# A first mixer whose gate row and next modulation move to ScalarE and GpSimd, and whose second output projection takes split weights

## Chip, core and metric

The kernel runs on one core of one Trainium2 chip. The metric is the device time of one execution in microseconds (us), lower is better. TensorE is called PE here, VectorE DVE, ScalarE ACT, GpSimd POOL, and SyncE, which issues nearly all loads, SP.

## What is computed

Two transformer blocks run one after the other on 256 tokens of width 1024. The change touches only the front of the first one:

```python
shift, scale, gate = ada_modulation(c, ada_w[l, s], ada_b[l, s])   # silu(c) @ w + b, in three parts; gate is 1 + the third
h = x * (1 + scale) + shift
y = mixer_ab(h, ...)                    # two attentions side by side, concatenated, @ w_out
x = layer_norm(alpha * x + gate * y, ...)
shift, scale, gate = ada_modulation(c, ada_w[l, s + 1], ada_b[l, s + 1])
h = x * (1 + scale) + shift             # enters the first MLP
```

mixer_ab holds a sliding-window attention ("a", with sinks) and a top-64 attention ("b"): for "b" an index score picks 64 keys for each token, and those scores must be finished before its mask exists. Both outputs, 512 columns each, go through one 1024x1024 projection. Everything is fp32.

## The kernel before

**Weights** come in chunks of 128x2048 fp32 (1 MB). Class Stream keeps them in one list in the order of use. A load is issued on SP up to three chunks ahead into one of four buffers "raw"; a chunk is then taken apart in pieces when the program needs it (need, get). Three kinds of chunk matter. A split chunk is turned into whi on ACT (L157, a rounded copy) and wlo on DVE (L158, the rest), and a product then takes three fp32r matmuls (L227 whi with x high, L228 wlo with x high, L229 whi with x low). A native chunk (f32=True) is loaded straight into buffers and multiplied in fp32 (L234). A modulation chunk has the transposed ada weights, and ada_piece (L436) multiplies 128x1024 of it by the row csil = silu(c) and sums along the row, in one DVE instruction.

**The order** on each engine is fixed when the program is built: a scheduler merges the pieces with the work around them. hold says that some chunks' pieces are issued only after a given instruction, here after the second selection mask.

**The front of the program** goes so. Modulation 0 (shift and scale) is summed on DVE. The projections in0, uq, in1 follow. Then come the index scores: six scores on PE, relu on ACT (L907, tile rl), weighted sums into isc on DVE (L913). select takes the 64 best by eight rounds of MAX (L925) and MATCH_REPLACE (L928) for each of two token tiles and ends with the mask smask (L947). Twelve attention units follow, six of "b" and six of "a". A unit is scores (L490, L496), a row maximum on DVE (L498), exponentials on ACT (L509), scaling on DVE (L526), transposes (L534), an evacuation on ACT (L536) and the product with v (L544, L549). Window's work for "a" (projection in2, keys, rope) stands after the first unit.

**The gate row** of modulation 0 is made on PE before: ada_products (L444) multiplies each 1024-wide gate row chunk, cut in four strips, by the column ccol; 32 calls of four strips' matmuls gather eight chunks in one PSUM tile. ada_gate adds the bias (L452, tile grow), spreads the row over the partitions by eight fp32 matmuls (L457) and writes the tile gate (L459). **Modulation 1** (chunks ada 1,0 to 1,7) is 16 DVE instructions L436. The layer norm after the mixer needs gate; the transposes behind it need modulation 1.

**The output projection** (out_proj) runs the half of "b" first, with split chunks about 2 and 3. These products fill PE between the units. The half of "a", chunks about 0 and 1, is native: 16 fp32 products L234 at the end of the mixer, held back by tail so that token tile 0 is finished first.

Of the kernel before, what the change touches and what calls it, by code (L numbers as in the profile page):

```python
# [8 lines left out]
F32 = DT.float32  # L9
# [187 lines left out]
class Kern:  # L197
# [242 lines left out]
    def ada_products(self, raw, ps, kt, o, n):  # L440

        def pc():
            for g in range(4):
# [4 lines left out]
    def ada_gate(self, ps, gate):  # L448

        nc = self.nc  # L450
        row = self.pa.tile([128, 256], F32, tag="grow", name="grow", bufs=1)
        nc.vector.scalar_tensor_tensor(row, ps[:, 0:256], 1.0, self.gate_b, op0=ALU.add, op1=ALU.add)  # L452
        for h in range(2):
            p = self.ps("o")
            for q in range(2):
                g = 32 * (2 * h + q)
                nc.tensor.matmul(p[:, q * 256:q * 256 + 256], self.ident[:, g:g + 1].to_broadcast([128, 128]),  # L457
                                 row, start=True, stop=True)
            nc.scalar.activation(gate[:, h * 512:h * 512 + 512], p, AF.Copy, scale=1.0 / ALPHA)  # L459
# [295 lines left out]
    def mixer_ab(self, gate, early):  # L755
# [3 lines left out]
        for i in range(2):  # L759
# [9 lines left out]
        self.ccol = self.pa.tile([128, KT, 32], F32, tag="ccol", name="ccol")  # L769
        nc.gpsimd.tensor_tensor(self.ccol, self.col("c", 0, 8)[:, :, None].to_broadcast([128, KT, 32]),  # L770
                                e[:, :, None].to_broadcast([128, KT, 32]), op=ALU.mult)
        self.gate_b = self.pa.tile([128, 256], F32, tag="gate_b", name="gate_b")
# [13 lines left out]
        for kt in range(KT):  # L786
# [19 lines left out]
            for t in range(2):  # L806
                k = kt % 4
                self.mm(p0[t][:, :456], (xT[:, kt, t * 128:t * 128 + 128],), wt, slice(k * 456, k * 456 + 456),
                        kt == 0, kt == KT - 1)

# [42 lines left out]

        def keysT(src, kT):

            nc.gpsimd.memset(kT[0:64, :, 1, :], 0.0)
            nc.gpsimd.memset(kT[64:128, :, 0, :], 0.0)
# [26 lines left out]
        kTb = self.px.tile([128, 2, 2, 256], F32, tag="tm", name="kTb", bufs=8)  # L884
        keysT(kd, kTb)
# [67 lines left out]
        def unit(t, heads, qk, mask, scale, v, op, base, done, sink=None):  # L953
# [4 lines left out]
            def s2(pT):  # L958
# [4 lines left out]
                if heads[-1] == 7:  # L963
                    ts = slice(t * 128, t * 128 + 128)
                    p3 = op[0].rearrange("p (a b) -> p a b", a=4)
                    if base == 1:
                        if base not in oT:
                            oT[base] = [self.px.tile([128, 4, 256], F32R, tag="tm", name=self.nm("oT"), bufs=8)
                                        for _ in range(2)]
                        self.split_evac(oT[base][0][:, :, ts], oT[base][1][:, :, ts], p3)  # L970
                    else:
                        if base not in oT:
                            oT[base] = [self.px.tile([128, 4, 256], F32, tag="tm", name=self.nm("oT"), bufs=8)]
                        nc.scalar.activation(oT[base][0][:, :, ts], p3, AF.Copy)
# [32 lines left out]
        for g in range(4):  # L1007
            nc.sync.dma_start(self.gate_b[32 * g:32 * g + 32, :],
                              A["rows"][ROWS["gate_b"]:ROWS["gate_b"] + 1, 256 * g:256 * g + 256].to_broadcast([32, 256]))
# [46 lines left out]
        def hook(i):  # L1056
            if i == 0:
                window()
                S.need(S.index["ada00g", 3])
            if i == 5:  # L1060
                self.ada_gate(self.strips, gate)
# [558 lines left out]
    def schedule_items(self):  # L1620
# [15 lines left out]
        def strips():  # L1636

            if self.strips is None:
# [325 lines left out]
```

## Time and profile before

| | us |
|---|---|
| runs, median (lowest to highest of 3) | 1337.09 (1335.97 to 1338.56) |
| the profiled execution | 1336.42 |
| its span in the trace | 1334.5 |
| PE busy in the span | 1289.8 (97%) |
| DVE busy | 1006.6 (75%) |
| ACT busy | 708.1 (53%) |
| POOL busy | 43.8 (3%) |

The table is read from the bottom: POOL is nearly idle over the whole span, ACT about half, while PE is busy nearly all the time. Shares of a whole span hide stages, so the argument below goes by stretches of the first 160 us: the profile's slices show PE below nine tenths nowhere but in the first two and the last.

### The profile page before, as it was taken

What the parts mean: (1) busy time and instruction counts of PE and PEld (TensorE: products, weight loads), DVE (VectorE), ACT (ScalarE), POOL (GpSimd) and SP (SyncE); (2) the same over time, 40 slices, a digit from 0 to 9 for tenths busy, and PEclk for the clock granted to TensorE, in tenths of its full rate; (3) what the DMA queues carried; (4) which work ended last, traced back from release to release, by engine and by line L of the source; (5) the groups of instructions that cost most, each with busy time, mean ns of one, the idle gap of its engine ahead of it and who ended that gap; (6) DMA issues with size and microseconds to landing.
All of it is one profiled execution on the core that took longest, in us unless ns stands there. A gap on an engine that the chain in (4) does not pass through costs nothing.

```text
span 1334.5 us, 18965 instructions
## 1 busy us (share of the span) xinstructions
PE 1289.8 (97%) x6970; PEld 1051.4 (79%) x6970; DVE 1006.6 (75%) x2048; ACT 708.1 (53%) x1532; POOL 43.8 (3%) x74
## 2 busy tenths in 40 slices
PE   5899999999999999999999999999999999999997
PEld 2356688888787788888699988888888877888886
DVE  7789999976999698666798778666677555766664
ACT  3245645554566665555543437555566754755552
POOL 2000000000100000000010000000000000000000
PEclk9999999999999999999999999999999999999999
DMA  9639689974457468555343334555534333455530
GB/s 363 252 146 332 248 299 347 343 272 158 180 202 281 158 217 300 188 191 178 109 158 116 138 127 170 188 185 188 189 139 158 126 127 126 174 189 189 190 127 32
DMA packets 39023, 260.21 MB, mean 195 GB/s; under 512 B 4625, under 2 KB 5009, under 8 KB 9362
## 3 DMA queue, kind: packets, MB, share of 16 engines
q1 hardware_dynamic: 38786, 258.47, 53.8%
q8 instruction: 55, 0.90, 0.3%
q0 software_dynamic: 144, 0.52, 0.1%
q14 instruction: 38, 0.31, 0.1%
HBM read 257.93 MB, written 1.05 MB: 194 GB/s over the span
## 4 chain that ended last, share of the span: by engine, by line
PE 73%; issue 11%; DVE 8%; ACT 3%; DMA 3%; POOL 2%; SPq 0%; POOLq 0%; DVEq 0%; ACTq 0%
PE acc L229 11%; PE acc L227 11%; PE acc L228 11%; PE scr L250 6%; PE o L250 6%; PE scr L251 3%; PE o L251 3%; PE scr L496 3%; PE acc L234 2%; DVE wlo L158 2%; DMA raw<-in_ada_dram 2%; PE o L534 1%; PE scr L229 1%; DVE junk L436 1%; POOL sm L258 1%
## 5 line engine op out<-in xcount | busy, mean ns | idle before, releaser
L158 DVE TENSOR_TENSOR wlo<-raw,whi 128x512 fp32r<-128x512 f32 x724 | 471.2, 686 | 129.8 <-ACT whi L157 119.9
L157 ACT ACTIVATE whi<-raw 128x512 fp32r<-128x512 f32 x724 | 418.9, 626 | 211.3 <-PE acc L229 87.7
L227 PE MATMUL acc<-whi,hh 128*128 128x512 f32 x512 | 201.2, 394 | 0.0
L228 PE MATMUL acc<-wlo,hh 128*128 128x512 f32 x512 | 201.2, 393 | 0.0
L229 PE MATMUL acc<-whi,hl 128*128 128x512 f32 x512 | 200.1, 392 | 0.0
L250 PE MATMUL scr<-xT,whi 128*128 128x512 f32 x464 | 166.8, 398 | 0.0
L250 PE MATMUL o<-xT,whi 128*128 128x512 f32 x464 | 166.1, 397 | 0.0
L251 PE MATMUL o<-xT,wlo 128*128 128x256 f32 x464 | 130.5, 281 | 0.0
L251 PE MATMUL scr<-xT,wlo 128*128 128x256 f32 x464 | 130.4, 281 | 0.0
L227 PEld LDWEIGHTS acc<-whi,hh 128*128 128x128 f32 x512 | 96.2, 188 | 22.9 <-ACT hh L737 1.3
L229 PEld LDWEIGHTS acc<-whi,hl 128*128 128x128 f32 x512 | 96.2, 188 | 22.1 <-DVE hl L738 0.8
L436 DVE SCALAR_TENSOR_TENSOR junk<-raw,csil 128x1024 bf16<-128x1024 f32 x88 | 108.6, 1234 | 6.2 <-DMA raw<-in_ada_dram 5.8
L228 PEld LDWEIGHTS acc<-wlo,hh 128*128 128x128 f32 x512 | 96.2, 188 | 18.6
L250 PEld LDWEIGHTS o<-xT,whi 128*128 128x128 f32 x464 | 87.1, 188 | 21.0
L250 PEld LDWEIGHTS scr<-xT,whi 128*128 128x128 f32 x464 | 87.1, 188 | 20.7 <-issue 0.5
L251 PEld LDWEIGHTS scr<-xT,wlo 128*128 128x128 f32 x464 | 87.5, 189 | 2.7 <-issue 0.5
L251 PEld LDWEIGHTS o<-xT,wlo 128*128 128x128 f32 x464 | 87.6, 189 | 0.0
L737 ACT ACTIVATE hh<-f 128x512 fp32r<-128x512 f32 x58 | 36.7, 633 | 86.8 <-DVE f L736 86.7
L731 ACT ACTIVATE r<-scr 128x256 f32<-128x256 f32 x58 | 22.3, 384 | 96.6 <-PE scr L251 96.6
L732 DVE TENSOR_TENSOR r<-scr,r 128x256 f32<-128x256 f32 x58 | 24.6, 424 | 55.7 <-ACT r L731 55.4
L738 DVE TENSOR_TENSOR hl<-f,hh 128x512 fp32r<-128x512 f32 x58 | 40.1, 691 | 33.3 <-ACT hh L737 33.1
L229 PE MATMUL acc<-whi,xT 128*128 128x512 f32 (+1 forms) x176 | 63.4, 361 | 0.7 <-DVE xT L306 0.5
(398 smaller groups left out, 2294.9 us busy)
## 6 DMA issues: line engine op xcount, KB each, us to landing
raw<-in_m_w_dram SPq DMA_DIRECT2D x128, 1024.0 KB, 4.8
raw<-in_ada_dram SPq DMA_DIRECT2D x48, 1024.0 KB, 5.4
raw<-in_c_qk_dram SPq DMA_DIRECT2D x8, 1024.0 KB, 4.9
raw<-in_h_qf_dram SPq DMA_DIRECT2D x8, 1024.0 KB, 4.8
raw<-in_mla_o_dram SPq DMA_DIRECT2D x8, 1024.0 KB, 4.8
raw<-in_c_v_dram SPq DMA_DIRECT2D x4, 1024.0 KB, 4.7
raw<-in_c_w_out_dram SPq DMA_DIRECT2D x4, 1024.0 KB, 4.8
raw<-in_h_i_dram SPq DMA_DIRECT2D x4, 1024.0 KB, 5.0
```

What stands on the lines that cost most here:

```text
L157: nc.scalar.activation(hi, raw[:, a:b], AF.Copy)
L158: nc.vector.tensor_tensor(lo, raw[:, a:b], hi.bitcast(F32), op=ALU.subtract)
L227: mm(ps, xh, wh, start=start, stop=False)
L228: mm(ps, xh, wl, start=False, stop=False)
L229: mm(ps, xl, wh, start=False, stop=stop)
L234: self.nc.tensor.matmul(ps, x[0], w(c), start=start, stop=stop)
L250: mm(ps.rearrange("p (a b) -> p a b", a=2), w.h(c), x, start=start, stop=False)
L251: mm(ps[:, n:2 * n], w.l(c), x[:, 0, :], start=False, stop=stop)
L436: nc.vector.scalar_tensor_tensor(junk, raw[:, j * 1024:(j + 1) * 1024], 1.0, self.csil, op0=ALU.mult, op1=ALU.mult, accum_out=acc[:, n:n + 1])
L496: nc.tensor.matmul(o, q, k, start=False, stop=(i == len(ops) - 1))
L737: nc.scalar.activation(hh, f, AF.Copy)
L738: nc.vector.tensor_tensor(hl, f, hh.bitcast(F32), op=ALU.subtract)
```

## The change

Four edits, all in the front of the program:

- The gate row: for each of eight 128x1024 pieces ACT multiplies by one column of ccol (tile prod, two buffers in turn) and POOL adds the result to the tile gate, which is set to 1/32 on 32 partitions and to the bias on one of the others at first. Two fp32 matmuls with a matrix of ones then sum over partitions (ada_gate).
- Modulation 1: for each of 16 pieces POOL multiplies by csil into prod, and ACT copies prod onto itself and sums it. These chunks now stand ahead of the output projection's in the list, and are outside hold.
- Chunks about 0 and 1 are split, and the output of "a" too (split_evac); out_proj takes three fp32r matmuls everywhere.
- The zeroing of the key tiles (POOL) moves ahead of the new POOL work, the need of the gate's chunks ahead of the first attention unit, the need of the last modulation chunk to unit 3, and the bias row's load is one row instead of four broadcasts.

```diff
-    def ada_products(self, raw, ps, kt, o, n):
...
-                self.nc.tensor.matmul(ps()[32 * g:32 * g + 32, 0:n], self.ccol[:, kt, :],
-                                      raw[:, o + g * n:o + g * n + n], start=kt == 0, stop=kt == KT - 1)
+    def ada_rows(self, raw, kts):
...
+                w = self.prod[kt % 2]
+                nc.scalar.activation(w, raw[:, q * 1024:q * 1024 + 1024], AF.Identity, scale=self.ccol[:, kt:kt + 1])
+                nc.gpsimd.tensor_tensor(self.grow, self.grow, w, op=ALU.add)
...
+    def ada_piece2(self, raw, j, acc, n):
...
+            w = self.prod[j]
+            nc.gpsimd.tensor_tensor(w, raw[:, j * 1024:(j + 1) * 1024], self.csil, op=ALU.mult)
+            nc.scalar.activation(w, w, AF.Copy, accum_out=acc[:, n:n + 1])
...
-        row = self.pa.tile([128, 256], F32, tag="grow", name="grow", bufs=1)
-        nc.vector.scalar_tensor_tensor(row, ps[:, 0:256], 1.0, self.gate_b, op0=ALU.add, op1=ALU.add)
...
+            nc.tensor.matmul(p, self.ones, self.grow[:, h * 512:h * 512 + 512], start=True, stop=True)
...
+        self.grow = gate
+        self.prod = [self.pa.tile([128, 1024], F32, tag="prod", name="prod"), self.tm("prod")]
...
-                        nc.scalar.activation(oT[base][0][:, :, ts], p3, AF.Copy)
...
+                    self.split_evac(oT[base][0][:, :, ts], oT[base][1][:, :, ts], p3)
...
-        S.hold(("ada00g", 0), 4, 16, [self.sel_last[1]])
+        S.hold(("about", 2), 0, 16, [self.sel_last[1]])
...
+        keys_zero(kTa)
+        S.need(S.index["ada00g", 3])
...
-                S.need(S.index["ada00g", 3])
+            if i == 3:
+                S.need(S.index["ada", 1, 7])
...
+        for j in range(8):
+            ada(1, j)
         for j in range(4):
-            S.add(("about", (j + 2) % 4), A["ab_w_out"][(j + 2) % 4], 2048, f32=j >= 2)
-            ada(1, 2 * j)
-            ada(1, 2 * j + 1)
+            S.add(("about", (j + 2) % 4), A["ab_w_out"][(j + 2) % 4], 2048)
```

Where the new pieces come to stand decides what waits for them. The first place is ACT's queue at the exponentials of the first attention unit (tile pt). hT is the evacuated query of "b" and "a", akd and av are keys and values of "a". Before:

```order
L851 ACTIVATE hT<-o_491 128x4x128
L851 ACTIVATE hT<-o_503 128x4x128
L509 ACT_TABLE_LOAD
L509 ACTIVATE pt_613,sm_614<-scr_605,sm_611 128x128 x4
L1029 ACTIVATE av_652<-acc_625 128x128
L873 ACTIVATE akd_649<-kr_642 128x2x64 x2
```

The same place on ACT in the changed kernel; L459 are the sums of modulation 1, on the two buffers prod and prod_171 in turn:

```order
L864 ACTIVATE hT<-o_493 128x4x128
L864 ACTIVATE hT<-o_505 128x4x128
L459 ACTIVATE prod_171,adaacc_89<-prod_171 128x1024
L459 ACTIVATE prod,adaacc_89<-prod 128x1024
L518 ACT_TABLE_LOAD
L518 ACTIVATE pt_633,sm_634<-scr_625,sm_631 128x128 x4
L459 ACTIVATE prod_171,adaacc_89<-prod_171 128x1024
L459 ACTIVATE prod,adaacc_89<-prod 128x1024
L459 ACTIVATE prod_171,adaacc_89<-prod_171 128x1024
L888 ACTIVATE akd_669<-kr_662 128x2x64 x2
L1039 ACTIVATE av_672<-acc_645 128x128
```

Five sums stand ahead of the first exponentials and eleven behind: the two shown ahead of the table load are the fourth and fifth of sixteen, the three behind it the sixth to eighth.

The second place is ACT's queue between the fourth unit's exponentials (the first row, pt_788 before and pt_772 now) and the first split of about 2 (whi). Before, that split's first half is already done here:

```order
L509 ACTIVATE pt_788,sm_789<-scr_781,sm_786 128x256 x2
L272 ACTIVATE oT_807<-o_776 128x4x128
L509 ACTIVATE pt_818,sm_819<-scr_811,sm_816 128x256 x2
L536 ACTIVATE pT_831<-o_826 128x512
L157 ACTIVATE whi_1151<-raw_1121 128x512 x2
```

Now:

```order
L518 ACTIVATE pt_772,sm_773<-scr_765,sm_770 128x256 x2
L459 ACTIVATE prod_171,adaacc_89<-prod_171 128x1024
L459 ACTIVATE prod,adaacc_89<-prod 128x1024
L545 ACTIVATE pT_834<-o_829 128x512
L459 ACTIVATE prod_171,adaacc_89<-prod_171 128x1024
L459 ACTIVATE prod,adaacc_89<-prod 128x1024
L272 ACTIVATE oT_840<-o_760 128x4x128
L459 ACTIVATE prod_171,adaacc_89<-prod_171 128x1024
L518 ACTIVATE pt_851,sm_852<-scr_844,sm_849 128x256 x2
L545 ACTIVATE pT_864<-o_859 128x512
L518 ACTIVATE pt_878,sm_879<-scr_871,sm_876 128x256 x2
L157 ACTIVATE whi_1155<-raw_810 128x512 x2
```

The last of the sixteen sums now stands directly ahead of the fifth unit's exponentials (pt_851), and all of about's splits stand behind it.

## Rows read from the trace of the kernel before

**Rows 1.** Stretches: length, then busy time and count by engine, PE clock, DMA.

```profile
40.00:55.00 15.00, 11.94 (x44) 6.13 (x45) 9.12 (x30) 6.14 (x15) 1.54 (x3) 0.89 0.94 379
55.00:83.60 28.60, 28.57 (x91) 15.99 (x89) 24.72 (x89) 5.67 (x14) 0.00 (x0) 1.00 0.00 0
83.60:98.90 15.30, 13.09 (x112) 7.55 (x112) 13.59 (x40) 10.69 (x34) 0.00 (x0) 1.00 0.77 310
98.90:144.10 45.20, 45.06 (x228) 26.75 (x226) 42.51 (x120) 26.09 (x78) 0.86 (x1) 1.00 0.85 310
```

**Rows 2.** Timeline of DVE: start, duration (us), engine, line, operation, tiles; index scores and selection.

```profile
52.23 2.74 DVE L913 SCALAR_TENSOR_TENSOR isc<-rl,iw,isc 128x128 f32<-128x128 f32 x7
...
64.45 0.30 DVE L925 MAX8 sm<-mr 128x8 f32<-128x128 f32 x1
...
66.60 0.29 DVE L925 MAX8 sm<-mr 128x8 f32<-128x128 f32 x1
...
70.94 0.41 DVE L947 CAST smask<-eq 128x512 bf16<-128x512 f32 x1
...
78.34 0.43 DVE L947 CAST smask<-eq 128x512 bf16<-128x512 f32 x1
78.68 0.68 DVE L498 TENSOR_REDUCE sm<-scr 128x4 f32<-128x512 f32 x1
```

**Rows 3.** Timeline of ACT: third relu, first exponentials, fifth unit's exponentials.

```profile
53.96 0.60 ACT L907 ACTIVATE rl<-scr 128x512 f32<-128x512 f32 x1 [0.73 <-PE scr L903]
...
80.94 0.37 ACT L509 ACTIVATE pt<-scr,sm 128x128 f32<-128x128 f32 x1
...
82.23 0.21 ACT L509 ACTIVATION_READ_ACCUMULATOR pt<-scr,sm 128x1 f32 x1
...
98.89 0.49 ACT L509 ACTIVATE pt<-scr,sm 128x256 f32<-128x256 f32 x1
...
134.00 6.33 ACT L157 ACTIVATE whi<-raw 128x512 fp32r<-128x512 f32 x12
```

**Rows 4.** Timeline of POOL: every two-input instruction of 128x1024 in the trace.

```profile
197.57 2.72 POOL L470 TENSOR_TENSOR diag<-cst,adamod 128x1024 f32<-128x1024 f32 x1 [44.73 <-DVE adamod L463]
...
342.97 1.89 POOL L470 TENSOR_TENSOR diag<-cst,adamod 128x1024 f32<-128x1024 f32 x1
...
514.66 2.13 POOL L470 TENSOR_TENSOR diag<-cst,adamod 128x1024 f32<-128x1024 f32 x1 [45.62 <-DVE adamod L463]
```

**Rows 5.** Timeline of DVE: what ran beside those three, and two undisturbed rows.

```profile
143.46 0.55 DVE L588 TENSOR_SCALAR r<-r,sm,sm 128x512 f32<-128x512 f32 x1 [0.44 <-POOL sm L258]
...
198.46 0.42 DVE L732 TENSOR_TENSOR r<-o,r 128x256 f32<-128x256 f32 x1
198.79 2.58 DVE L436 SCALAR_TENSOR_TENSOR junk<-raw,csil 128x1024 bf16<-128x1024 f32 x1
...
201.30 0.68 DVE L736 SCALAR_TENSOR_TENSOR f<-r 128x512 f32<-128x512 f32 x1
...
343.03 2.11 DVE L588 TENSOR_SCALAR r<-r,sm,sm 128x512 f32<-128x512 f32 x1 [0.44 <-POOL sm L258]
...
514.95 2.39 DVE L736 SCALAR_TENSOR_TENSOR f<-r 128x512 f32<-128x512 f32 x1
```

**Rows 6.** Groups of PE from 83 to 88.5 us: busy us, mean ns.

```profile
L444 PE MATMUL acc<-raw,ccol 128*32 128x256 f32 x56 | 4.0, 384 | 0.0
```

**Rows 7.** Timeline of PE: start-to-start spacing of split and native products.

```profile
106.60 0.39 PE L228 MATMUL acc<-wlo,oT 128*128 128x512 f32 x1
106.83 0.40 PE L229 MATMUL acc<-whi,oT 128*128 128x512 f32 x1
...
139.51 1.02 PE L234 MATMUL acc<-whi,oT 128*128 128x512 f32 x2
140.37 1.02 PE L234 MATMUL acc<-wlo,oT 128*128 128x512 f32 x2
...
142.94 1.02 PE L234 MATMUL acc<-whi,oT 128*128 128x512 f32 x2
```

**Rows 8.** Groups of DVE from 90 to 134.5 us.

```profile
L436 DVE SCALAR_TENSOR_TENSOR junk<-raw,csil 128x1024 bf16<-128x1024 f32 x16 | 19.5, 1218 | 0.1
```

More of the change, by code (lines that the diff above doesn't have):

```diff
@@ L438, in ada_piece, with piece, pc, ada_gate @@
         return pc
[L440 removed]
+    def ada_rows(self, raw, kts):
+        nc = self.nc
+        def piece(q, kt):
+            def pc():
+                w = self.prod[kt % 2]
+                nc.scalar.activation(w, raw[:, q * 1024:q * 1024 + 1024], AF.Identity, scale=self.ccol[:, kt:kt + 1])
+                nc.gpsimd.tensor_tensor(self.grow, self.grow, w, op=ALU.add)
+            return pc
+        return [piece(q, kt) for q, kt in enumerate(kts)]
+    def ada_piece2(self, raw, j, acc, n):
+        nc = self.nc
         def pc():
[L443 to L445 removed]
+            w = self.prod[j]
+            nc.gpsimd.tensor_tensor(w, raw[:, j * 1024:(j + 1) * 1024], self.csil, op=ALU.mult)
+            nc.scalar.activation(w, w, AF.Copy, accum_out=acc[:, n:n + 1])
         return pc
[L448 removed]
+    def ada_gate(self, gate):
         nc = self.nc
[L451 to L452 removed]
         for h in range(2):
             p = self.ps("o")
[L455 to L458, printed above, removed]
+            nc.tensor.matmul(p, self.ones, self.grow[:, h * 512:h * 512 + 512], start=True, stop=True)
             nc.scalar.activation(gate[:, h * 512:h * 512 + 512], p, AF.Copy, scale=1.0 / ALPHA)
@@ L768, in mixer_ab @@
         nc.scalar.activation(e, self.col("c", 0, 8), AF.Sigmoid)
[L769 to L772, printed above, removed]
+        self.ccol = self.pa.tile([128, KT], F32, tag="ccol", name="ccol")
+        nc.gpsimd.tensor_tensor(self.ccol, self.col("c", 0, 8), e, op=ALU.mult)
+        self.grow = gate
+        self.prod = [self.pa.tile([128, 1024], F32, tag="prod", name="prod"), self.tm("prod")]
+        for a, b, v in ((0, 32, 0.0), (32, 64, 1.0 / 32), (64, 128, 0.0)):
+            nc.gpsimd.memset(gate[a:b, :], v)
         self.adab = self.p1.tile([128, 96], F32, tag="adab", name="adab")
@@ L809, in mixer_ab @@
                         kt == 0, kt == KT - 1)
+        nc.sync.dma_start(gate[0:1, :], A["rows"][ROWS["gate_b"]:ROWS["gate_b"] + 1, :])
         cqT = self.pa.tile([128, 2, 256], F32, tag="cqT", name="cqT", bufs=1)
@@ L965, in s2 @@
                     p3 = op[0].rearrange("p (a b) -> p a b", a=4)
[L966 to L973, printed above, removed]
-                        nc.scalar.activation(oT[base][0][:, :, ts], p3, AF.Copy)
+                    if base not in oT:
+                        oT[base] = [self.px.tile([128, 4, 256], F32R, tag="tm", name=self.nm("oT"), bufs=8)
+                                    for _ in range(2)]
+                    self.split_evac(oT[base][0][:, :, ts], oT[base][1][:, :, ts], p3)
                     done(t)
@@ L1058, in hook @@
                 window()
-                S.need(S.index["ada00g", 3])
+            if i == 3:
+                S.need(S.index["ada", 1, 7])
             if i == 5:
-                self.ada_gate(self.strips, gate)
+                self.ada_gate(gate)
             if i == 11:
@@ L1634, in schedule_items @@
         S.add(("abin", 2, 0), A["ab_in2"], 2048, f32=True)
-        def strips():
-            if self.strips is None:
-                self.strips = self.ps("acc")
-            return self.strips
-        self.strips = None
         def gate0(j):
             def fn(raw):
-                return [self.ada_products(raw, strips, 2 * j + q, 1024 * q, 256) for q in range(2)]
+                return self.ada_rows(raw, (2 * j, 2 * j + 1))
             S.add(("ada00g", j), A["ada"][8 + j], 2048, fn=fn)
@@ L1652, in fn @@
                 if j < 8:
-                    ps = [self.ada_piece(raw, 0, acc, j), self.ada_piece(raw, 1, acc, 8 + j)]
+                    f = self.ada_piece2 if i == 1 else self.ada_piece
+                    ps = [f(raw, 0, acc, j), f(raw, 1, acc, 8 + j)]
                 else:
```

7 lines of the change are left out of this document (3 added, 4 removed).

## The prediction

> **What bounds the kernel now.** I read the stretches first [rows 1], then the timelines of DVE and ACT through the front of the program [rows 2, 3], then PE's spacing [rows 7]. Three stages stand out. From 55 to 83.6 us no load moves and POOL does nothing; PE counts as busy, but the first exponentials at 80.94 wait for DVE, which works through index scores and selection without a gap worth naming and reaches the first unit's row maximum only at 78.68 [rows 2, 3]. From 83.6 to 98.9 PE has holes (13.09 busy of 15.30) and carries the gate products. From 98.9 to 144.1 PE is busy for 45.06 of 45.20 us: the tail is PE's, with DVE close behind (42.51). Behind that the MLPs keep PE full, so a shift of the mixer's end reaches the end of the span whole. So DVE's selection sets the beginning, PE the tail.
>
> **What the new POOL work costs.** The change gives POOL 24 two-input instructions of 128x1024, 8 additions and 16 products. The trace has three of that shape [rows 4]: one runs unhindered in 1.89 us; the other two took 2.72 and 2.13 because DVE was in the middle of a two-input instruction, and from the end of that they took about 1.85. All of their inputs repeat one operand along a dimension, the new ones do not, so 1.89 may be low. I take 1.89: 24 x 1.89 = 45.4 us, on a single engine, in a row. An addition on GpSimd of twice that length is given as 4497 ns by the Trainium skill (GPSIMD Engine Reference, section Elementwise — side-by-side cycle accounting). By half of it, an estimate of 2.25 us, the 24 would take 54 us and the sum below would be some 8 us higher; the rows are nearer the case.
>
> **What it does to DVE.** The same three rows show the second cost [rows 4, 5]. The scaling L588 takes 0.55 us alone and 2.11 when it began 0.06 us after POOL's instruction. L736 takes 0.68 alone and 2.39 right behind a POOL start. The ada product L436, 1.218 us on average [rows 8], took 2.58 and ended 1.08 us after POOL did. In each case DVE stood still until POOL had finished, and POOL waited likewise for the DVE instruction that was running. L732, which has one of its inputs in PSUM, ran beside POOL in its usual 0.42. So a DVE instruction with two SBUF inputs, or a plain scaling out of SBUF, and a POOL instruction of this kind exclude each other.
>
> The Trainium skill says the same of one shared port pair (SBUF — State Buffer, section Who interferes with whom) and goes further: a DVE instruction with one SBUF input outside the fast modes does not contend. No row here has a MAX or MATCH_REPLACE beside a running POOL instruction; if they did contend, against that page, the first term below would be 7 us larger.
>
> **First term, the first exponentials.** In the changed order five of the sixteen sums of modulation 1 stand on ACT ahead of the first exponentials, and POOL's buffers alternate: its 16th instruction must wait for the sum that stands right behind those exponentials. So up to 15 POOL instructions fall into the stretch in which DVE makes scores and masks, and they start early: raw chunks are there by 55 us, ACT's first multiplication follows the first relu (the third now ends at 54.56), so POOL starts near 55. DVE has 34 instructions in that stretch that exclude POOL (2 rope sums, 2 scalings, 14 accumulations L913, 2 masked copies, and 7 in each selection's end), most of them alone between instructions that do not. Each gap lets POOL in, and the next one waits for it. 15 x 1.89 = 28.4 us. Hidden are: POOL's share beside the MAX and MATCH_REPLACE run at 64.45 to 66.9 (2.5 us); some 13 single gaps of 0.3 us [rows 2], 3.9; and the queries' rope, which reads PSUM, with the waits of ACT for rl, some 3. Left: 28.4 - 9.4 = 19 us. The low end is 0 (POOL always fits into DVE's gaps), the high end 28. I take 19, since all three rows show the full wait. PE meanwhile stands at the first mask and the projection in2 (L234) waits behind it on PE; that is late with the mask and ready with it. PE's clock may fall in that pause; it was at 0.89 on average in the stretch from 40 to 55 that has pauses too. I leave that in the upper end.
>
> **Second term, from the first to the fifth unit's exponentials.** Before: 82.4 to 98.9, 16.5 us [rows 3], in which PE has 4.0 us of gate products [rows 6] that go away. Now nine POOL instructions (16 to 24) and their sums lie in it, since the last sum stands ahead of the fifth exponentials. 9 x 1.89 = 17.0; each waits for a DVE instruction of about 0.3, 2.7; and at three places POOL waits for a sum that is queued on ACT behind a unit's exponentials, about 1.5 each, 4.5. Together 24.2, that is 7.7 more than before. The bounds are 1 (only the nine) and 13. The gate products' 4 us are lost in it: they were on PE's path, and this path is longer.
>
> **Third term, the tail.** The native products are 16 at 0.86 us spacing; a split one is 3 x 0.233 = 0.70 [rows 7]. 16 x 0.16 = 2.6 us gained on the engine that bounds the tail. The unit before's score is done earlier, 1 us. Against it: about 2 is loaded only when POOL has freed the fifth chunk of modulation 1 and split only behind the last sum, so PE's filler comes some 4 us after the fifth exponentials instead of with them, and other PE work covers about 2.5 of that: 1.5 us lost. Together -2. What else is edited has cover: DVE loses 16 x 1.218 = 19.5 us [rows 8] and gains 8 splits and two evacuations, about 7; DVE's load falls in a stage where PE bounds, so this brings nothing by itself, and would if DVE were the limit there. ACT gains 24 instructions of about 1.0 to 1.2 us and 8 splits, up to 33 us, in a stretch of 89 us (55 to 144) where it is busy 42 [rows 1]; it fits on average, and what it delays in its queue is counted in the second term. The gate's spread is the same number of columns. SP's loads: the bias row is one instead of four, with nothing urgent behind; the modulation chunks now load into the quiet stretch from 55 to 83.6, which relieves the stretch behind it, but there PE bounds. The MLP's first weights, split from 134 on before [rows 3], keep their cover behind the tail.
>
> **Sum.** 19 + 7.7 - 2 = 24.7 us. The profiled execution is 1336.4 (its span 1334.5 and 1.9 around it), the runs' median 1337.1; 1336.4 + 24.7 = 1361.
>
> **Rivals.**
> (a) POOL is slow but shuts nobody out for long: DVE keeps its pace, POOL starts at 55 and needs 45.4, so it ends at 100.4 at the earliest, some 104 with ACT's waits; a sum of 1.2 us more and the fifth exponentials come at 105 instead of 98.9, 6.5 late. With -2 from the tail the time is 1341. For it: the selection has many one-input instructions; POOL could get its turns there. Against it: rows 5.
> (b) The other side. POOL's instructions take 1.6 us or less and lie in gaps, so all are done before 95. Then the second stretch is PE's, without the gate products, and the tail has split products: 4.0 + 2.6 = 6.6 us less, 1330. It decides at (95 - 55) / 24 = 1.66 us for an instruction with all its waits. Nothing in rows 4 is under 1.8.
> (c) Losses and gains cancel: POOL ends about 99 and only the fifth unit feels it, within 2.7 us of the time before, 1337.
> That the change does not do what it says is no rival: the order shows it.
>
> **How the numbers follow.** Forecast 0.71, at 1361, by its own terms 1347 to 1375; (a) 0.13; (b) 0.11; (c) 0.05. The range is 1338 to 1375: it leaves out (b), most of (c) and a top end in which POOL is slower than its rows or PE's clock falls, together under 0.2. 0.2% (2.7 us) is about what a measurement of this kernel can tell from no change: faster 0.11, same 0.05, slower 0.84.
>
> **What would show it.** In the changed profile POOL's 24 instructions should take 1.9 us or more each from about 55 to past 115, back to back up to the 15th, with a pause for the first exponentials. DVE's accumulations and mask steps should show rows of 1.5 to 2.5 us where they took 0.3 to 0.5. The second mask should come near 97 instead of 78.3, the fifth exponentials near 125 instead of 98.9; the tail behind them should be PE's and 2 us shorter. If masks come at 79 and POOL ends past 100, it is (a). If POOL's instructions are short, or DVE's rows beside them are as before, the first term falls and with it the forecast.

## The result and the profile of the changed kernel

The change makes the kernel slower: a median of 1373.24 us over four runs (1370.49 to 1374.52) against 1336.53 (1335.52 to 1338.56) for the kernel before on the same chip. The ratio is 1.0272, with a 95% interval of 1.0259 to 1.0285, so 36.7 us are lost. The forecast was 1361 with a range of 1338 to 1375: the side and the mechanism were right, the size of the loss was 12 us too small.

The traces of the two kernels give the three terms of the prediction. First POOL's timeline in the changed one: start, duration (us; of a joined row, the sum), line, operation, tiles, count, and in brackets the idle time before it and what ended it.

```profile
56.54 4.77 POOL L448 TENSOR_TENSOR gate<-gate,prod 128x1024 f32<-128x1024 f32 x2 [13.29 <-issue]
63.32 2.42 POOL L448 TENSOR_TENSOR gate<-gate,prod 128x1024 f32<-128x1024 f32 x1 [2.02 <-ACT prod L447]
67.90 12.35 POOL L448 TENSOR_TENSOR gate<-gate,prod 128x1024 f32<-128x1024 f32 x5 [2.15 <-ACT prod L447]
80.21 16.43 POOL L458 TENSOR_TENSOR prod<-raw,csil 128x1024 f32<-128x1024 f32 x7
109.67 9.38 POOL L458 TENSOR_TENSOR prod<-raw,csil 128x1024 f32<-128x1024 f32 x4 [13.03 <-ACT prod L459]
120.81 5.11 POOL L458 TENSOR_TENSOR prod<-raw,csil 128x1024 f32<-128x1024 f32 x2 [1.76 <-ACT prod L459]
130.24 7.03 POOL L458 TENSOR_TENSOR prod<-raw,csil 128x1024 f32<-128x1024 f32 x3 [4.32 <-ACT prod L459]
```

Fifteen instructions run before the first exponentials, then comes the pause of 13.03 us for the buffer that the 16th needs, then nine more. The order of events is the prediction's, but for two pauses of 2 us among the first eight and for one number: an instruction takes 2.4 us on average, not 1.89. POOL's groups from 50 to 150 us (busy us, mean ns of one, idle time before them):

```profile
L458 POOL TENSOR_TENSOR prod<-raw,csil 128x1024 f32<-128x1024 f32 x16 | 38.0, 2402 | 19.1 <-ACT prod L459 19.1
L448 POOL TENSOR_TENSOR gate<-gate,prod 128x1024 f32<-128x1024 f32 x8 | 19.1, 2393 | 17.9 <-issue 13.3 <-ACT prod L447 4.2
```

Next DVE's timeline in the same stretch, the answer to [rows 2].

```profile
70.54 0.27 DVE L944 MATCH_REPLACE8 mr<-sm,mr 128x128 f32<-128x128 f32 x1
70.73 2.31 DVE L929 SCALAR_TENSOR_TENSOR isc<-rl,iw,isc 128x256 f32<-128x256 f32 x1
72.97 0.28 DVE L941 MAX8 sm<-mr 128x8 f32<-128x128 f32 x1
...
78.17 2.23 DVE L932 COPY_PREDICATED isc<-cst,fill 128x128 f32<-128x128 int32 x1
...
82.92 2.07 DVE L951 TENSOR_SCALAR eq<-isc,sm 128x128 f32<-128x128 f32 x1
...
97.05 0.40 DVE L963 CAST smask<-eq 128x512 bf16<-128x512 f32 x1
...
104.44 0.43 DVE L963 CAST smask<-eq 128x512 bf16<-128x512 f32 x1
104.79 0.68 DVE L507 TENSOR_REDUCE sm<-scr 128x4 f32<-128x512 f32 x1
```

The same three steps before, as groups of DVE from 50 to 79.4 us:

```profile
L913 DVE SCALAR_TENSOR_TENSOR isc<-rl,iw,isc 128x256 f32<-128x256 f32 x7 | 3.3, 477 | 0.1
L916 DVE COPY_PREDICATED isc<-cst,fill 128x128 f32<-128x128 int32 x2 | 0.6, 292 | 0.0
L935 DVE TENSOR_SCALAR eq<-isc,sm 128x128 f32<-128x128 f32 x1 | 0.3, 281 | 0.0
```

POOL runs without a break from 67.90 to 96.64. In that time an accumulation L929 with two SBUF inputs takes 2.31 us where it took 0.48 before, a masked copy 2.23 for 0.29, a comparison of one tensor with a column 2.07 for 0.28: DVE stands until POOL's instruction is over. MAX8 and MATCH_REPLACE8, between them, keep their 0.27 to 0.28, so the 7 us that the prediction set aside for the other case are not there. The Trainium skill (SBUF — State Buffer, section Who interferes with whom) says of a DVE instruction with one SBUF input outside the fast modes that it does not contend; these two agree (the eight values of sm have a row of their own in the trace, MATCH_VALUE_LOAD). The first mask comes at 97.05 (70.94 before), the second at 104.44 (78.34). From 96.64 on POOL waits, and the second mask's steps take their usual time.

ACT's timeline, the answer to [rows 3]: the first exponentials, the last of the sixteen sums, and the fifth unit's exponentials.

```profile
107.05 0.37 ACT L518 ACTIVATE pt<-scr,sm 128x128 f32<-128x128 f32 x1
...
108.34 0.21 ACT L518 ACTIVATION_READ_ACCUMULATOR pt<-scr,sm 128x1 f32 x1
...
137.31 1.06 ACT L459 ACTIVATE prod<-prod 128x1024 f32<-128x1024 f32 x1 [0.72 <-POOL prod L458]
...
138.36 0.46 ACT L518 ACTIVATE pt<-scr,sm 128x256 f32<-128x256 f32 x1
```

And the stretches, as in [rows 1] (length; busy time and count of PE, PEld, DVE, ACT, POOL; PE's granted clock; DMA share; GB/s):

```profile
55.00:83.60 28.60, 19.00 (x51) 8.55 (x49) 27.94 (x46) 12.84 (x16) 22.50 (x10) 0.96 0.44 147
83.60:98.90 15.30, 1.39 (x4) 1.13 (x5) 15.20 (x23) 5.75 (x12) 13.04 (x6) 0.50 0.62 206
98.90:144.10 45.20, 28.83 (x109) 18.64 (x108) 39.07 (x77) 28.90 (x76) 21.53 (x9) 0.70 0.34 117
```

PE, busy for 13.09 of 15.30 us in the second stretch before, is busy for 1.39 now, since it waits for the mask; its granted clock falls to 0.50, the lower of its two levels (1.2 of 2.4 GHz). DVE is busy for 15.20 of 15.30, but two thirds of that is waiting for POOL.

The account, by the start of the first exponentials, that of the fifth unit's, PE's first transpose of the layer norm behind the mixer (L291), and the span:

| | first exponentials | fifth unit's | layer norm | span |
|---|---|---|---|---|
| before | 80.94 | 98.89 | 144.15 | 1334.5 |
| after | 107.05 | 138.36 | 181.38 | 1371.8 |
| later by | 26.1 | 39.5 | 37.2 | 37.3 |

The layer norm's rows, before and after:

```profile
144.15 0.63 PE L291 MATMUL o<-cst,r 128*128 128x128 f32 x4 [0.19 <-DVE sm L590]
```

```profile
181.38 0.63 PE L291 MATMUL o<-cst,r 128*128 128x128 f32 x4 [0.58 <-DVE sm L599]
```

So the first term is +26.1, the second 39.5 - 26.1 = +13.4, the third 37.2 - 39.5 = -2.3. What is lost by the layer norm is lost at the end of the span too. Of the 26.1, the two traces are 1.2 us apart already at 40 us, ahead of any of this work (DVE's first cn starts at 39.66 before and at 40.83 after). The changed order gives about as much back: in the run below without POOL's instructions the first exponentials come at 79.65.

### The profile page after: what moved, and what is told of

Its sections match the earlier page's. It is cut to its first block, busy times and chain, and to the rows that moved or that the text cites. A ratio compares the mean times of both kernels' runs of the same rounds, so it can differ in the third digit from the quotient of the medians.

```text
span 1371.8 us, 18908 instructions
## 1 busy us (share of the span) xinstructions
PE 1288.1 (94%) x6911; PEld 1055.1 (77%) x6918; DVE 1037.4 (76%) x2025; ACT 738.5 (54%) x1580; POOL 103.0 (8%) x101
## 3 DMA queue, kind: packets, MB, share of 16 engines
HBM read 257.80 MB, written 1.05 MB: 189 GB/s over the span
## 4 chain that ended last, share of the span: by engine, by line
PE 79%; DVE 13%; ACT 3%; DMA 2%; issue 1%; POOL 1%; SPq 0%; DVEq 0%; POOLq 0%; ACTq 0%
PE acc L227 13%; PE acc L229 13%; PE acc L228 12%; PE o L250 8%; PE scr L250 8%; PE o L251 4%; PE scr L251 4%; PE scr L505 2%; DMA raw<-in_ada_dram 2%; DVE isc L929 1%; PE o L543 1%; POOL sm L258 1%; DVE wlo L158 1%; PE acc L1359 1%; PE scr L229 1%
## 5 line engine op out<-in xcount | busy, mean ns | idle before, releaser
L157 ACT ACTIVATE whi<-raw 128x512 fp32r<-128x512 f32 x732 | 423.4, 626 | 213.3 <-PE acc L229 88.6
L258 POOL TENSOR_TENSOR sm<-rsq,mhalf 128x1 f32<-128x1 f32 (+2 forms) x26 | 19.2, 737 | 1007.3 <-DVE rsq L257 1007.3
L436 DVE SCALAR_TENSOR_TENSOR junk<-raw,csil 128x1024 bf16<-128x1024 f32 x72 | 89.1, 1237 | 7.5 <-DMA raw<-in_ada_dram 7.1
L746 ACT ACTIVATE hh<-f 128x512 fp32r<-128x512 f32 x58 | 36.7, 632 | 87.1 <-DVE f L745 87.1
```

The costliest lines, as they stand in the source:

```text
L157: nc.scalar.activation(hi, raw[:, a:b], AF.Copy)
L258: nc.gpsimd.tensor_tensor(out, v, self.mhalf[:, :n], op=ALU.pow)
L436: nc.vector.scalar_tensor_tensor(junk, raw[:, j * 1024:(j + 1) * 1024], 1.0, self.csil, op0=ALU.mult, op1=ALU.mult, accum_out=acc[:, n:n + 1])
L746: nc.scalar.activation(hh, f, AF.Copy)
```

## The experiments

All spans below are to be read against 1334.5 of the kernel before; where a ratio stands, it is to runs of that kernel on the same chip.

**POOL's time and nothing else.** To the kernel before, 15 products are added that nobody reads; only the first waits for anything:

```diff
         sc = [index_scores(t) for t in range(2)]
+        for i in range(15):
+            nc.gpsimd.tensor_tensor(gate, iqT.rearrange("p a b -> p (a b)") if i == 0 else self.csil, self.csil, op=ALU.mult)
```

> The kernel before with 15 POOL products of 128x1024 added, whose result nobody reads; the first starts when the index queries are there, about 54 us. ACT, PE, the loads and all else are as before. Theory (POOL shuts DVE out while it runs, whoever waits for POOL): first exponentials late by 15 x 2.35 - 9 = 26 us, at 107; what follows is as before: 1360 to 1364. Rival (the loss came with ACT's work, the loads or a wait for POOL's results): no one waits for these, 1336 to 1338.

Measured: 1356.81 us, ratio 1.0150 (1.0129 to 1.0170). POOL's groups, a DVE row beside them, and the first exponentials:

```profile
L995 POOL TENSOR_TENSOR gate<-csil 128x1024 f32<-128x1024 f32 x14 | 27.6, 1969 | 1.0
L995 POOL TENSOR_TENSOR gate<-iqT,csil 128x1024 f32<-128x1024 f32 x1 | 2.4, 2368 | 10.3 <-ACT iqT L851 10.3
```

```profile
80.80 1.91 DVE L913 SCALAR_TENSOR_TENSOR isc<-rl,iw,isc 128x256 f32<-128x256 f32 x1
```

```profile
101.91 0.37 ACT L509 ACTIVATE pt<-scr,sm 128x128 f32<-128x128 f32 x1
```

The rival falls: work that nobody waits for delays the first exponentials by 21.0 us, and the span by 20.4. The size misses the expectation because both operands of 14 of them are the same tile: these take 1.97 us, where the one with two different tiles takes 2.37. With the measured 27.6 + 2.4 = 30.0 us the theory's own sum is 30.0 - 9 = 21.0.

**Half the length.** Each of POOL's instructions works on 512 of 1024 columns:

```diff
-                nc.gpsimd.tensor_tensor(self.grow, self.grow, w, op=ALU.add)
+                nc.gpsimd.tensor_tensor(self.grow[:, :512], self.grow[:, :512], w[:, :512], op=ALU.add)
...
-            nc.gpsimd.tensor_tensor(w, raw[:, j * 1024:(j + 1) * 1024], self.csil, op=ALU.mult)
+            nc.gpsimd.tensor_tensor(w[:, :512], raw[:, j * 1024:j * 1024 + 512], self.csil[:, :512], op=ALU.mult)
```

> The changed kernel with each of POOL's 24 instructions on 512 of its 1024 columns; all else, ACT's 24 of 1024 too, is the same. Left out: half of the products and additions of gate row and modulation 1. Theory (POOL's instruction time, 2.35 us, times 24 in a row): about 1.2 us each; first exponentials late by 15 x 1.2 = 18 less 9 hidden, so 9 instead of 26; first to fifth exponentials 9 x 1.2 = 10.8 and 6 of pauses and 2.3 at the ends, 19 instead of 29.9; tail as in the changed kernel: about 9 more than before, 1342 to 1350. Rival (ACT's 24 instructions, which stay whole, or the waits between the engines set the pace): at most 5 us less than the changed kernel, 1368 or more.

Measured: 1348.89 us, ratio 1.0094 (1.0076 to 1.0113), inside the theory's band. One group of five, and the first exponentials:

```profile
72.32 6.42 POOL L458 TENSOR_TENSOR prod<-raw,csil 128x512 f32<-128x512 f32 x5
```

```profile
91.55 0.37 ACT L518 ACTIVATE pt<-scr,sm 128x128 f32<-128x128 f32 x1
```

At 1.28 us each here (1.32 on average over all 24) the first exponentials are late by 10.6 us, and 24.4 of the 36.7 us are gone, with all of ACT's work unchanged. So the loss follows POOL's time.

**One repeated operand.** The price was the number that was wrong, so the products' second operand is read from one column:

```diff
-            nc.gpsimd.tensor_tensor(w, raw[:, j * 1024:(j + 1) * 1024], self.csil, op=ALU.mult)
+            nc.gpsimd.tensor_tensor(w, raw[:, j * 1024:(j + 1) * 1024], self.csil[:, 0:1].to_broadcast([128, 1024]), op=ALU.mult)
```

> The changed kernel with the second operand of POOL's 16 products read from one column, repeated along the row, instead of from 1024 columns. The products' values are therefore not the reference's. Theory (the prediction took 1.89 us from instructions with repeated operands; three full streams cost 2.35): the products take 1.89 us or near it, the additions still 2.4, and the time falls by some 16 x 0.45 = 7 us, 1364 to 1368. Rival (the price has another reason, such as ACT or a DMA using the buffers beside it): 2.3 us each, 1371 to 1374.

Measured, in one run: 1367.73 us, inside the theory's band. POOL's groups here:

```profile
L458 POOL TENSOR_TENSOR prod<-raw,csil 128x1024 f32<-128x1024 f32 x16 | 30.4, 1927 | 19.2 <-ACT prod L459 19.2
L448 POOL TENSOR_TENSOR gate<-gate,prod 128x1024 f32<-128x1024 f32 x8 | 19.2, 2394 | 19.3 <-issue 14.7 <-ACT prod L447 4.2
```

1.93 us with a repeated operand, 2.39 with two full streams in the same run: that is nearly the whole gap between the prediction's 1.89 and the changed kernel's 2.40.

**Instructions that read nothing.** In place of each two-input instruction POOL fills the same buffer twice:

```diff
-            nc.gpsimd.tensor_tensor(w, raw[:, j * 1024:(j + 1) * 1024], self.csil, op=ALU.mult)
+            for _ in range(2):
+                nc.gpsimd.memset(w, 0.0)
```

(and likewise for the additions)

> The changed kernel with each of POOL's 24 two-input instructions replaced by two fills of the same 128x1024 buffer, which read nothing; places and waits in POOL's queue and all of ACT's work stay. Left out: the additions and products. A fill of 32x1024 took 0.98 us at the start of the changed kernel, so POOL is busy for about 2 us each time instead of 2.35. Theory A (only POOL instructions that read SBUF shut DVE out): DVE's accumulations and mask steps take their 0.3 to 0.5 us, first exponentials at 81 to 84; POOL's chain from 55 ends near 105, so the fifth exponentials come up to 8 us late: 1334 to 1345. Theory B (any POOL instruction on SBUF shuts it out): first exponentials late by 15 x 2 - 9 = 21, in all 25 to 31 more than before: 1361 to 1367.

Measured: 1341.66 us, ratio 1.0035 (1.0019 to 1.0051): theory A. POOL's groups, and three DVE rows beside an unbroken run of fills:

```profile
L460 POOL MEMSET prod<- 128x1024 f32 x32 | 30.4, 972 | 7.5 <-ACT prod L461 6.6
```

```profile
70.45 0.33 DVE L958 SCALAR_TENSOR_TENSOR cum<-cum,sm,eq 128x128 f32<-128x128 f32 x1
...
71.63 0.80 DVE L962 TENSOR_SCALAR eq<-gt 128x128 f32<-128x128 f32 x1
...
72.67 0.27 DVE L963 TENSOR_TENSOR eq<-eq,cst 128x128 f32<-128x128 f32 x1
```

POOL is busy for 1.95 us at each place, as long as with a product of a repeated operand, but DVE's two-input instructions take their usual 0.27 to 0.33; the first exponentials come at 84.70. Only a few one-input steps wait for a fill (0.80 for 0.2). What shuts DVE's two-input steps out is POOL's reading, not its being busy.

**Instructions that read one tensor.**

```diff
-                nc.gpsimd.tensor_tensor(self.grow, self.grow, w, op=ALU.add)
+                nc.gpsimd.tensor_scalar(self.grow, w, 1.0, None, op0=ALU.mult)
...
-            nc.gpsimd.tensor_tensor(w, raw[:, j * 1024:(j + 1) * 1024], self.csil, op=ALU.mult)
+            nc.gpsimd.tensor_scalar(w, raw[:, j * 1024:(j + 1) * 1024], 1.0, None, op0=ALU.mult)
```

> The changed kernel with each of POOL's 24 two-input instructions replaced by a multiplication by the constant 1 of the one input (ACT's product, or the raw chunk). Left out: additions and products. Theory A (an instruction that reads even one tensor shuts DVE out; a fill, which reads none, cost 4.8 us in all): DVE's accumulations beside it take POOL's duration, and with 1.0 to 1.9 us each the time is 1346 to 1362. Theory B (only two-input instructions shut it out): DVE keeps its 0.3 to 0.5 us and the time is as with the fills, 1338 to 1343.

Measured, in one run: 1362.85 us, and both theories miss. POOL's group, DVE's accumulations as a group, and the row at which DVE then waits:

```profile
L458 POOL TENSOR_SCALAR prod<-raw 128x1024 f32<-128x1024 f32 x16 | 44.2, 2788 | 0.8 <-ACT prod L459 0.8
```

```profile
L929 DVE SCALAR_TENSOR_TENSOR isc<-rl,iw,isc 128x256 f32<-128x256 f32 x7 | 4.7, 666 | 0.0
```

```profile
92.56 0.69 DVE L507 TENSOR_REDUCE sm<-scr 128x4 f32<-128x512 f32 x1 [7.45 <-PE scr L505]
```

The one-input instruction takes longer than the two-input one, 2.79 us. Yet DVE's accumulations average 0.67 us, where the changed kernel has 1.85 and the kernel before 0.48: a partial hindrance (two of the seven take 1.29 and 1.05, the others 0.46 to 0.47). What decides which ones wait is not shown. The second mask is ready at 84.7, but the first exponentials come at 96.7, since PE waits for the queries hT, which ACT copies behind its third sum, and that sum waits for POOL. So POOL's slowness reaches the path by the other road too, through ACT's queue.

**One half of the change at a time.** First the gate row alone on POOL, modulation 1 on DVE behind the selection:

```diff
-                    f = self.ada_piece2 if i == 1 else self.ada_piece
+                    f = self.ada_piece
...
-        S.hold(("about", 2), 0, 16, [self.sel_last[1]])
+        S.hold(("ada00g", 0), 4, 16, [self.sel_last[1]])
```

> The changed kernel with modulation 1 back on DVE as in the kernel before, held behind the selection; the gate row stays on ACT and POOL, the split stays. POOL has 8 instructions left. Theory (a POOL instruction and the DVE instructions of scores and masks exclude each other): the 8 additions alone make DVE late by what they made it late in the changed kernel up to the masked copy, 80.3 against 64.1, so 16 us; first exponentials at 97; behind them the stretch to the fifth exponentials is as before or up to 4 us shorter (no gate products on PE), the tail 2 us shorter: 10 to 14 more than before, 1347 to 1351. Rival: the delay comes from the products with DVE's two-input modulation gone, or from ACT, and the additions only fill waits: first exponentials at 81 to 84, time 1331 to 1337.

Measured: 1356.68 us, ratio 1.0151 (1.0137 to 1.0165), more than expected. The first exponentials and the stretch behind them:

```profile
93.77 0.37 ACT L518 ACTIVATE pt<-scr,sm 128x128 f32<-128x128 f32 x1
```

```profile
93.80:119.30 25.50, 17.52 (x77) 9.97 (x75) 23.99 (x64) 12.04 (x40) 0.00 (x0) 0.80 0.54 187
```

Eight additions (19.1 us) delay the first exponentials by 12.8 us; the rival falls. But the next stretch takes 25.5 us instead of 17.95, with POOL idle: DVE is busy for 23.99 of it, because the demand for the whole of modulation 1 after the fourth unit (L1070 of the changed kernel's code, the diff's S.need on ("ada", 1, 7)) now puts 11 products of 1.22 us on DVE ahead of the fifth unit's exponentials, where the kernel before has one. That order is part of the change too.

Then modulation 1 alone on POOL, the gate's products back on PE:

```diff
-            return self.ada_rows(raw, (2 * j, 2 * j + 1))
+            return [self.ada_products(raw, strips, 2 * j + q, 1024 * q, 256) for q in range(2)]
```

> The changed kernel with the gate row back on PE as in the kernel before; modulation 1 stays on POOL and ACT, the split stays. POOL has 16 instructions left. The gate's chunks keep the raw buffers until PE has used them, at about 84 to 88. Theory (one serial POOL chain decides when the fifth unit's exponentials come): first exponentials at 81 as before, the first product at about 89, then 16 x 2.35 = 37.6 and 6 of pauses, the last sum at 133 to 137; the fifth exponentials 34 to 38 later than before, the tail 2 shorter: 32 to 36 more than before, 1368 to 1373, nearly all of the changed kernel's loss. Rival (the two groups each cost their share of POOL's time): 16 of 24 instructions, two thirds of 36.7: 24 more, about 1361; or, if the products only matter where they meet the selection, the gate's share of 16 is gone and 20 more stay, about 1357.

Measured: 1363.85 us, ratio 1.0207 (1.0192 to 1.0223), 27.7 more: under the theory's band, and above the rival's. POOL's first product and ACT's exponentials of the first, fifth and seventh unit:

```profile
90.28 2.35 POOL L454 TENSOR_TENSOR gate<-raw,csil 128x1024 f32<-128x1024 f32 x1 [47.12 <-DMA raw<-in_ada_dram]
```

```profile
80.59 0.37 ACT L519 ACTIVATE pt<-scr,sm 128x128 f32<-128x128 f32 x1
...
115.56 0.46 ACT L519 ACTIVATE pt<-scr,sm 128x256 f32<-128x256 f32 x1
...
137.61 0.36 ACT L519 ACTIVATE pt<-scr,sm 128x128 f32<-128x128 f32 x1
```

The time does not decide here; the rows do. The first exponentials are not late at all, so the selection is untouched, and the loss is that of a chain that starts at 90.28 and whose last sum ends near 131.8. The expectation was too high because in this kernel the fifth unit's exponentials stand among the sums, not behind the last one; the first units after it wait for the end (137.6 against 107.1 before).

**The split alone.** About 0 and 1 and the outputs split, in the kernel before:

```diff
-            S.add(("about", (j + 2) % 4), A["ab_w_out"][(j + 2) % 4], 2048, f32=j >= 2)
+            S.add(("about", (j + 2) % 4), A["ab_w_out"][(j + 2) % 4], 2048)
```

(with the outputs' split as in the change)

> The kernel before with one part of the change alone: about 0 and 1 as split weights and the second output projection's outputs split; gate row and modulation 1 stay as before. Theory (the third term: the tail behind the fifth exponentials is PE's, and 16 native products at 0.86 us become 16 at 3 x 0.233): 2.2 to 2.6 us less than before, about 1334.3. Rival: DVE, busy for 42.51 of the tail's 45.20 us before, now also splits 8 pieces of 0.69 us and two outputs and becomes the limit: 42.5 + 6.5 = 49.0, 3 to 4 us more than before, about 1340.

Measured: 1342.26 us, ratio 1.0047 (1.0034 to 1.0060): the rival is right in its sign and its cause, though 6.1 us are more than its 3 to 4, and the third term's reason was wrong. The tail, and PE's row at its end:

```profile
98.80:148.80 50.00, 43.22 (x246) 30.08 (x244) 46.97 (x128) 30.62 (x86) 0.86 (x1) 0.98 0.78 277
```

```profile
148.84 2.00 PE L291 MATMUL o<-cst,r 128*128 128x128 f32 x8 [6.83 <-DVE sm L590]
```

PE has fewer busy us (43.22 against 45.06 [rows 1]) but waits for 6.83 us for DVE, which now has 46.97.

**Is it DVE?** The 16 scalings of the last six units' probabilities go to ACT, with the split and without:

```diff
-                return self.attn_scores(t, heads, qk, m, scale, sink)
+                return self.attn_scores(t, heads, qk, m, scale, sink, norm_act=base == 0)
```

> The kernel before with the split of about 0 and 1 and of the outputs (which alone took 6.1 us more), and with the 16 scalings of the last six units' probabilities (0.31 us each) moved from DVE to ACT. Theory (the split fails because DVE is the limit in the tail, where PE waited 6.83 us for it): DVE loses 16 x 0.31 = 5.0 us and gets back under PE: 5 less than with the split alone, 1336 to 1338. Rival (the limit is in the order of DVE's last instructions, or ACT, which gains 16 x 0.4, becomes the limit): 1341 or more.

> The kernel before with the 16 scalings of the last six units' probabilities moved from DVE to ACT, and nothing else. Theory (the tail before is PE's, 46.4 of 46.6 us busy, and DVE is only close behind): no change, 1335 to 1338. Rival (DVE is the limit there and PE's busy time hides waits): 3 to 5 us less, about 1332.

Measured: with the split 1338.20 us, ratio 1.0007 (0.9997 to 1.0016); without it 1337.38, ratio 1.0005 (0.9995 to 1.0014). The first is at the upper edge of what the theory gave, the second inside it. Each against the kernel before on its own chip, the split cost 6.1 us and 1.3 are left with the scalings moved, so some 5 come back; without the split the move brings nothing. With both, PE still waits for DVE in the tail, for less long:

```profile
145.29 0.63 PE L291 MATMUL o<-cst,r 128*128 128x128 f32 x4 [2.62 <-DVE sm L590]
```

From the fifth exponentials to that row DVE is as busy as before (42.60 us against 42.56) and PE less (42.95 against 45.07), and the stretch is no shorter (45.57 against 45.26). So PE and DVE both bound that tail: to relieve one of them alone brings nothing.

**The change without POOL.** What would it be worth if POOL's work were free?

```diff
-                nc.gpsimd.tensor_tensor(self.grow, self.grow, w, op=ALU.add)
...
-            nc.gpsimd.tensor_tensor(w, raw[:, j * 1024:(j + 1) * 1024], self.csil, op=ALU.mult)
-            nc.scalar.activation(w, w, AF.Copy, accum_out=acc[:, n:n + 1])
+            nc.scalar.activation(w, raw[:, j * 1024:(j + 1) * 1024], AF.Copy, accum_out=acc[:, n:n + 1])
```

> The changed kernel without POOL's 24 instructions; ACT's 8 multiplications and 16 sums stay (the sums read the raw chunk). Left out: the additions of the gate row and the products of modulation 1. Theory (POOL is the whole loss, and what DVE and PE are relieved of is a gain): first exponentials at 81 as before, the stretch behind them up to 4 us shorter, the tail 2 to 2.6 shorter: 5 to 6.6 less than before, 1330 to 1332, which is what rival (b) of the prediction gave. Rival (ACT's 28 us of new work and the order of loads cost on their own): 1337 or more, so that a part of the loss is not POOL's.

The same, with the demand for all of modulation 1 ahead of the fifth unit taken out:

```diff
-            if i == 3:
-                S.need(S.index["ada", 1, 7])
```

> The kernel without POOL's instructions (1335.5), and without the demand that all of modulation 1 be issued before the fourth unit's end: the last sums then stand behind the fifth unit's exponentials in ACT's queue instead of ahead of them. Left out, as there: the additions and products. Theory (of the 6.6 us that PE is relieved of, ACT's sums in front of the exponentials gave back most): 2 to 4 us less than with the sums ahead, 1331 to 1334. Rival (the relief itself is small, since PE's gate products filled waits): no change, 1335 to 1337.

Measured: 1335.51 us, ratio 0.9991 (0.9981 to 1.0000), and 1334.43, ratio 0.9982 (0.9972 to 0.9991). Both lie between the theory's band and the rival's. POOL's instructions are thus the whole loss: without them nothing of it is left. But the gain behind them is 1.4 to 2.4 us, not 6.6. Between the two the step is 1.1 us, and both intervals overlap: that ACT's sums give back most of the relief isn't shown. In the first of them PE has these two waits behind the first exponentials, where the timeline of the kernel before shows none until 93.45:

```profile
84.71 0.33 PE L874 MATMUL o<-cst,akd 128*128 128x128 f32 x1 [1.92 <-ACT akd L886]
87.18 0.90 PE L874 MATMUL o<-cst,akd 128*128 128x128 f32 x3 [2.14 <-ACT akd L886]
```

The copies akd stand behind three sums of 1.06 us in ACT's queue. The 4.0 us of gate products [rows 6] are off PE, and PE waits instead. Its granted clock is 0.81 from 80.5 to 98.9 us there, where it was 1.00 before, so a part of the missing gain may be the clock's; no run separates the two.

No version that computes all that the kernel before does beats it.

## Why the prediction came out as it did

**What bounds the kernel.** Right for the first part: DVE sets the first exponentials, as the unread products show. For the tail, "the tail is PE's, with DVE close behind" was right as it stood, but the sum used only its first half.

**POOL's price.** This is the mis-sized term. It was taken as 1.89 us; the changed kernel has 2.39 and 2.40 on average. The prediction named the reason it might be low (the three instructions in [rows 4] repeat an operand along a dimension, the new ones do not) and took it all the same. The run with a repeated operand shows that reason: 1.93 against 2.39. The Trainium skill's figure (GPSIMD Engine Reference, section Elementwise — side-by-side cycle accounting), halved to an estimate of 2.25, was nearer than the rows. POOL's 24 instructions took 35.5 us ahead of the first exponentials and 21.5 behind, 57.0 in all for 45.4 in the sum: 11.6 of the 12 us that were missing.

**The range.** It held the time, but only by its top end, and in part by luck: the prediction counts a POOL slower than its rows among what the range leaves out, and just that came. It fitted in because the bounds of the first two terms were set wide for another reason, the overlap. Those bounds (0 to 28, 1 to 13, with the -2) give 1335 to 1375; the lower end of 1347 "by its own terms" doesn't follow from them.

**DVE shut out.** Right, and the best number of the sum was the least certain: what hides. The prediction put 9.4 of 15 instructions' time under cover. POOL's busy time ahead of the first exponentials less their delay:

| | POOL busy, 15 instructions | delay | hidden | extra time in DVE's rows |
|---|---|---|---|---|
| changed kernel | 35.5 | 26.1 | 9.4 | 26.1 |
| repeated operand | 32.4 | 23.7 | 8.7 | 23.0 |
| unread products | 30.0 | 21.0 | 9.0 | 21.4 |
| half the length | 19.5 | 10.6 | 8.9 | 10.4 |

The delays hold the 0.6 to 1.6 us by which these traces start late against that of the kernel before (DVE's first cn) and, but for the unread products, what the changed order gives back. The last column is free of both: it sums what the same rows of DVE, from the first score to the second mask, take longer than before. By either the hidden time is about 9 us. That the changed kernel hides the forecast's 9.4 to the tenth is luck: of its three parts the one with the queries' rope fell away, since the rope is over at 56.29, before POOL's first addition at 56.54. The single gaps hid more than 0.3 us instead: most of POOL's 2.4 us instructions make a row of DVE only 1.7 to 1.9 us longer. So the first term fails by its price alone: 35.5 - 28.4 = 7.1 us, and 19 + 7.1 = 26.1.

**First to fifth exponentials.** The chain is the forecast one, link by link: from the end of the first exponentials at 108.55, POOL's start 1.1 us later, 21.5 of POOL (17.0 was said), 6.1 of pauses at two places instead of three (4.5 and 2.7 were said for pauses and for DVE), and 1.1 for the last sum. Together 29.8, against 24.2; before it was 16.5. Of the 5.6 us missing, 4.5 are again the price; the ends of the chain add 2.2, and the pauses, with DVE's share in them, are 1.1 shorter than was said.

**The tail.** Said -2, measured -2.3, and right for a reason that wasn't given. 16 native products saved are worth nothing while modulation 1 is on DVE: the split alone costs 6.1 us. In the change DVE is also rid of its 19.5 us of products, and it is then PE alone that bounds the tail (41.41 us of 43.00, DVE 34.66):

```profile
138.40:181.40 43.00, 41.41 (x230) 28.07 (x229) 34.66 (x100) 30.20 (x86) 0.55 (x1) 0.96 0.57 205
```

The term's other two parts, 1 us gained and 1.5 lost, no run separates. The sentence that the relief of DVE "brings nothing by itself" holds; that PE's 2.6 us could be counted by themselves does not.

**The gate's 4 us.** Said to be on PE's path and lost in a longer one. The runs without POOL don't bear out the first half: with nothing longer in the way, the stretch from the first to the fifth exponentials takes 20.1 and 18.9 us, not less than the 17.95 before. Whether the products filled waits, ACT's sums took their place, or PE's lower clock took the gain is open.

**The rivals.** (a) fails at DVE's rows, 2.3 us for 0.48. The gain of (b) is not there even in the kernel without POOL's instructions, which takes 1334 to 1336, not 1330. (c) has POOL end about 99; it ends at 137.27.

**PE's clock.** It fell to 0.50 while PE waited for the mask. With the unread products PE waits too, for 10.33 us, and the clock is 0.78 from 92.0 to 101.9, but behind the first exponentials all is as before:

```profile
101.90:118.90 17.00, 13.63 (x114) 7.69 (x113) 14.45 (x45) 12.16 (x42) 0.00 (x0) 1.00 0.73 279
```

From there to the fifth unit's it takes 17.0 us (17.95 before), and the span is later by no more than the first exponentials are. So the fall in that pause cost nothing there. In the changed kernel the clock stays low longer, 0.67 from 107.0 to 138.4. The chain that is late runs over POOL, DVE and ACT there, but its 6.1 us of pauses are for sums that stand in ACT's queue behind work that waits for PE and DVE; what part of them is the clock's no run separates.

## What to carry to other kernels

Before work goes from DVE to POOL, ask not only whether POOL has time but what DVE does meanwhile: in a stretch where DVE works on two SBUF inputs, a POOL instruction with two SBUF inputs can cost DVE nearly its own length, here 1.7 of 2.4 us on average, and a product that it takes over would have cost DVE 1.2. Price an instruction by a row with the same operand pattern, and if the rows at hand differ in it, put the forecast at the dearer end. Where two engines are both full in a stage, count the relief of one only together with that of the other.

## What was not expected of the hardware

- A POOL product of 128x1024 fp32 takes 2.36 to 2.40 us on average with two full operands, 1.93 with one repeated from a single column, 1.97 with the same tile twice; with 512 columns 1.32.
- A POOL multiplication of one tensor by a constant takes 2.79 us, longer than the product of two tensors, but it hinders DVE's two-input accumulations far less (0.67 us on average against 1.85).
- A POOL fill of 128x1024 takes 0.97 us and leaves DVE's two-input instructions alone. The Trainium skill says the same of a GpSimd instruction that only writes (SBUF — State Buffer, section Who interferes with whom); the run with fills agrees, with 0.27 to 0.33 us.
